# The order of the two maps in a differential attention, and a folded query scale

## The chip, the cores and the metric

The kernel runs on one core of a Trainium2 chip. The core has five engines with instruction queues of their own, each worked off in order: TensorE (PE, matrix products into PSUM), VectorE (DVE), ScalarE (ACT), GpSimd (POOL) and SyncE (SP, which here only issues DMA transfers). They wait for each other by semaphores. The metric is the device time of one launch in microseconds; a time is the median of several runs.

## The reference

Two layers of a diffusion backbone work on 512 latent tokens and 256 context tokens, each 1024 wide. Layer 0 has differential attention: 8 heads, each with two query and key parts of width 64, and the second softmax map is subtracted with a learned factor:

```python
lam = exp(sum(lp[0] * lp[1])) - exp(sum(lp[2] * lp[3])) + lam_init
o1 = sweep_attention(qq[..., 0, :], kk[..., 0, :], vv)
o2 = sweep_attention(qq[..., 1, :], kk[..., 1, :], vv)
o = rms_norm(o1 - lam * o2, subln_g) * (1.0 - lam_init)
return (o * silu(gate)) @ w_out
```

Layer 1 has grouped-query attention with 8 query heads and 2 key heads of width 128. Queries and keys go through an RMS norm per head (eps 1e-6) before rotation, and the scores are scaled by 128 ** -0.5. In both layers latent queries read latent and context keys, and context queries read context keys only. Around each mixer stand an adaLN shift, scale and gate, and norms before and after. All data are float32.

## The kernel before

The kernel keeps every product accurate by splitting each operand into a high and a low part and adding three matmuls (`mm3`: hi*hi, hi*lo, lo*hi; lines 146 to 148, or 153 for probabilities times values). ScalarE makes the high part by a cast, VectorE or POOL the low part by a subtraction.

**Layer 0.** For each of 8 heads: the projections of queries, keys, values and gate (L146 to L148) run as filling work between the attention of the head before. The attention of a head is made of score units, one for each block of 128 queries over 768 keys (`unit`), and for the two context blocks one joint unit over 256 keys (`unit_ctx`; the last head uses `unit` for them too). A unit holds two PSUM score tiles, one for each map, `sc[0]` and `sc[1]`; there are two such tiles in all, named `sc_72` and `sc_73` in the order, so the next unit can write only when the exponentials of the last have read them. Its twelve matmuls (L862, in the context unit L891) have only 64 contraction rows. Map 1 uses array rows 64 to 127 and map 0 rows 0 to 63, and the code gives them alternately, map 1 first.

Then follow, for map 0 and then map 1: the negated row maximum on VectorE (L867), the exponential with its row sum on ScalarE (L870), and the reciprocal of the sum on VectorE (L873). Map 0 is multiplied by its reciprocal on POOL (`scaled(EP0, ...)`, shown under the helper's line L208). For map 1 VectorE multiplies the reciprocal by `nlam`, the negated lambda (L877), and then computes p1 * r1 + p0 into map 0's buffer (L878). The context unit does the same in lines 897 to 909. The combined map is transposed on TensorE (L927), split into `ah` on ScalarE (L930) and `al` on VectorE (L931), and multiplied by the values (L153).

**Layer 1.** `q_proj` projects two query heads for 128 tokens at a time; `head_rstd` takes the sum of squares on ScalarE, and on POOL multiplies by 1/128, adds eps (L1270) and raises to the power of -0.5 (L1271). VectorE multiplies this by 128 ** -0.5 (L1341); the result is the per-row scale in the exponential (L1405) and of the maximum (L1402).

**What sets the order.** The generators of filling work and the steps of attention are given in an order by due times and lags (`Step`, `flow`). The framework then orders the instructions of each engine when the program is built, by priorities (`high_priority`) and by when it reckons that an instruction could start. The order is fixed from then on: at run time each engine takes its queue as it stands. A chain of order-only links (`after(prev)`) keeps the twelve matmuls of a unit in their order among themselves, but does not keep others out from between them.

Of the kernel before, what the change touches and what calls it, by code (L numbers as in the profile page):

```python
# [12 lines left out]
ALU = mybir.AluOpType  # L13
# [3 lines left out]
P = 128  # L17
# [3 lines left out]
C = 256  # L21
# [3 lines left out]
EPS = 1e-6  # L25
LAM_INIT = 0.8 - 0.6 * math.exp(0.0)
SC_A = 64 ** -0.5
SC_B = 128 ** -0.5
# [42 lines left out]
EP0 = 'p'  # L71
# [13 lines left out]
def tile_backbone(  # L85
# [20 lines left out]
    nc = tc.nc  # L106
# [97 lines left out]
    def scaled(eng, dst, src, s_):  # L204
        if eng == "a":
            nc.scalar.activation(dst, src, AF.Copy, scale=s_)
        else:
            (nc.vector if eng == "v" else nc.gpsimd).tensor_scalar(dst, src, s_, 1.0, ALU.mult, ALU.mult)  # L208
# [490 lines left out]
    with tc.tile_pool(name="t0", bufs=1) as t0:  # L699
# [140 lines left out]
        def s_units(h, qts):  # L840
            res = []

            def unit(qt):
                k0, nk = (0, T) if qt < NQ else (512, C)
                l, ps_ = small(2), []
                if nk == T:
                    sc = [sc2(), sc2()]
                else:
                    if h < KT - 1 or qt == NQ:
                        sts["sc"] = sc2()  # L850
                    sc = [sts["sc"]] * 2
                w = 384 if nk == T else 256
                qh, ql, kh_, kl_ = qk[h]
                tok = slice(qt * P, (qt + 1) * P)
                prev = None
                for j in range(nk // w):
                    c = slice(k0 + j * w, k0 + j * w + w)
                    for i, (a, b) in enumerate(((qh, kh_), (qh, kl_), (ql, kh_))):
                        for m in (1, 0):
                            r = slice(m * 64, m * 64 + 64)  # L860
                            with after(prev):
                                prev = nc.tensor.matmul(  # L862
                                    sc[m][:, j if nk == T else m, :w], a[r, tok], b[r, c], start=i == 0, stop=i == 2)
                for m in range(2):
                    scv = sc[m][:, :, :384] if nk == T else sc[m][:, m, :256]
                    mx = small()
                    nc.vector.tensor_reduce(mx, scv, AX.XY if nk == T else AX.X, ALU.max, negate=True)  # L867
                    pt = t0.tile([P, T], F32, tag=f"p{m}", name=nm("p"), bufs=4 if m == 0 else 2)[:, :nk]
                    pv_ = pt.rearrange("p (j n) -> p j n", j=2) if nk == T else pt
                    nc.scalar.activation(pv_, scv, AF.Exp, bias=mx, accum_out=l[:, m:m + 1])  # L870
                    ps_.append(pt)
                    r = l[:, m:m + 1]
                    nc.vector.reciprocal(r, r)  # L873
                    if m == 0:
                        scaled(EP0, pt, pt, r)
                    else:
                        nc.vector.tensor_tensor(r, r, nlam, ALU.mult)  # L877
                        nc.vector.scalar_tensor_tensor(ps_[0], pt, r, ps_[0], ALU.mult, ALU.add)  # L878
                        res.append(ps_[0])

            def unit_ctx():
                sc = [sc2(), sc2()]
                qh, ql, kh_, kl_ = qk[h]
                prev = None
                for qt in (NQ, NQ + 1):
                    tok = slice(qt * P, (qt + 1) * P)
                    for i, (a, b) in enumerate(((qh, kh_), (qh, kl_), (ql, kh_))):
                        for m in (1, 0):
                            r = slice(m * 64, m * 64 + 64)
                            with after(prev):  # L890
                                prev = nc.tensor.matmul(  # L891
                                    sc[m][:, qt - NQ, :C], a[r, tok], b[r, S:T], start=i == 0, stop=i == 2)
                l = [small(2), small(2)]
                pts = []
                for m in range(2):
                    mx = small(2)
                    nc.vector.tensor_reduce(mx, sc[m][:, :, :C], AX.X, ALU.max, negate=True)
                    pt = t0.tile([P, T], F32, tag=f"p{m}", name=nm("p"), bufs=4 if m == 0 else 2)
                    pts.append([pt[:, e * C:(e + 1) * C] for e in range(2)])
                    for e in range(2):  # L900
                        nc.scalar.activation(pts[m][e], sc[m][:, e, :C], AF.Exp, bias=mx[:, e:e + 1], accum_out=l[m][:, e:e + 1])
                    nc.vector.reciprocal(l[m], l[m])
                    if m:
                        nc.vector.tensor_tensor(l[m], l[m], nlam.to_broadcast([P, 2]), ALU.mult)
                    for e in range(2):
                        if m == 0:
                            scaled(EP0, pts[0][e], pts[0][e], l[0][:, e:e + 1])
                        else:
                            nc.vector.scalar_tensor_tensor(pts[0][e], pts[1][e], l[1][:, e:e + 1], pts[0][e], ALU.mult, ALU.add)
                res.extend(pts[0])  # L910

            if qts[0] == NQ and h < KT - 1:
                return res, [Step(unit_ctx, 1.0)]
            sts = {}
            cost = 1.2 if qts[0] < NQ else 0.5
            return res, [Step(lambda qt=qt: unit(qt), cost) for qt in qts]
# [97 lines left out]
        for which, o in enumerate((oq, ok)):  # L1014
            r = qr_tile()
# [222 lines left out]
    with tc.tile_pool(name="t1", bufs=1, side="right") as t1p:  # L1238
# [22 lines left out]
                    sinb[:, t, j * 64:j * 64 + 64].unsqueeze(1).to_broadcast([P, n, 64]), ALU.mult)  # L1261
            nc.gpsimd.tensor_tensor(dst.rearrange("p (h d) -> p h d", h=n), ta_, tb_, ALU.add)

        def head_rstd(o):
            ssq = small(2)
            for j in range(2):
                jk = t1p.tile([P, P], F32, tag="jk", name=nm("jk"), bufs=1)
                nc.scalar.activation(jk, o[:, j * P:(j + 1) * P], AF.Square, accum_out=ssq[:, j:j + 1])
            r = t1p.tile([P, 2], F32, tag="qrs", name=nm("qrs"), bufs=16)
            nc.gpsimd.tensor_scalar(r, ssq, 1.0 / P, EPS, ALU.mult, ALU.add)  # L1270
            nc.gpsimd.tensor_tensor(r, r, mhalf, ALU.pow)  # L1271
            return r

# [58 lines left out]
        def q_proj(p):  # L1332
            while not ws.has(2 * p, 2 * p + 1):
                yield None
            w = (ws.get(2 * p), ws.get(2 * p + 1))
            qr = []
            for m in range(NQ):
                o = pj(256)
                yield from proj_tok(o, w, m)
                qrs[p, m] = head_rstd(o)  # L1340
                nc.vector.tensor_scalar(qrs[p, m], qrs[p, m], SC_B, None, ALU.mult)  # L1341
                q = t1p.tile([P, 256], F32, tag="qt", name=nm("q"), bufs=9)
                rope_tok(q, o, m)
                close(o)
                qr.append(q)
            ws.release(2 * p, 2 * p + 1)
            qlate[p] = qr
            q_t[p] = clock[0]
# [304 lines left out]
```

## Time and profile before

| | |
|---|---|
| median of 3 runs | 853.01 us (852.29 to 855.05) |
| the profiled execution's own time | 849.65 us |
| its span, first to last instruction | 847.5 us |
| TensorE busy | 804.9 us |
| VectorE, ScalarE, POOL busy | 500.4, 457.3, 406.8 us |

In the trace the first 100 us are loading, the modulation and the first projections; 100 to 500 us are layer 0's attention with its projections; 500 to 600 us layer 0's output projection and the keys and values of layer 1; 600 to 745 us layer 1's attention with its query and gate projections; the rest is layer 1's end. A row of a timeline gives start, duration, engine, line, operation, tiles, shape and count, and in brackets the idle time of the engine before it and what ended that. Matmul durations overlap, so what a matmul takes of TensorE's queue is read from one start to the next. A row of the waits gives who waited for whom, the total in us, how often, and the longest. "wait for" is inferred from semaphore events.

### The profile page before, as it was taken

To read this page: it belongs to the slowest core of one execution; us is meant where nothing else is said; L and a number is where in the kernel's file an instruction comes from. 1 tells how busy PE (TensorE), PEld (TensorE's weight loads), DVE (VectorE), ACT (ScalarE), POOL (GpSimd) and SP (SyncE) were. 2 spreads that over 40 slices of the span, in tenths; PEclk is the share of its full clock that TensorE was granted. 3 is DMA by queue.
4 is the path that set the end of the run, shared out by engine and by line. 5 is a ranking of instruction groups with operands and counts; after the bars stand their busy time and mean duration, and the time that the engine had idled before them with its cause. 6 is when DMAs were issued, how large, how long until landed. Compare 5 with 4: busy or idle time off the path is not lost. (4 is left out here: it accounts for less than half of the span.)

```text
span 847.5 us, 14226 instructions
## 1 busy us (share of the span) xinstructions
PE 804.9 (95%) x5472; PEld 710.2 (84%) x5472; DVE 500.4 (59%) x897; ACT 457.3 (54%) x1001; POOL 406.8 (48%) x390
## 2 busy tenths in 40 slices
PE   7899999999999999999999999989999889899997
PEld 6668888788887898887988898779999779899986
DVE  4323666777667634675357952677357577665634
ACT  5323456655565635674555852565455556666731
POOL 4333555754456654555722311565777546534201
PEclk8699999999999999999999999999999999999999
DMA  9923120222142431323330043030233340210112
GB/s 301 355 96 111 67 73 27 75 75 75 38 148 77 137 101 63 112 76 100 125 100 26 26 142 107 10 123 26 75 101 100 102 147 1 75 50 26 51 49 100
DMA packets 41539, 77.76 MB, mean 92 GB/s; under 512 B 3584, under 2 KB 18688, under 8 KB 41472
## 3 DMA queue, kind: packets, MB, share of 16 engines
q1 hardware_dynamic: 38048, 71.71, 25.7%
q10 hardware_dynamic: 3424, 5.15, 1.7%
q8 instruction: 43, 0.70, 0.3%
q14 instruction: 24, 0.20, 0.1%
HBM read 70.56 MB, written 2.10 MB: 86 GB/s over the span
## 5 line engine op out<-in xcount | busy, mean ns | idle before, releaser
L146 PE MATMUL bk<-whi,h 128*128 128x256 f32 (+1 forms) x592 | 178.0, 303 | 6.5 <-DVE u L1185 3.6
L147 PE MATMUL bk<-wlo,h 128*128 128x256 f32 (+1 forms) x592 | 177.0, 300 | 0.2 <-DVE wlo L201 0.2
L148 PE MATMUL bk<-whi,h 128*128 128x256 f32 (+1 forms) x592 | 176.1, 300 | 0.7 <-DVE h L1223 0.6
L146 PE MATMUL bk<-h,whi 128*128 128x512 f32 (+2 forms) x416 | 147.6, 355 | 2.8 <-ACT sq L959 1.5
L201 POOL TENSOR_TENSOR wlo<-raw,whi 128x1024 fp32r<-128x1024 f32 x46 | 110.4, 2406 | 74.3 <-ACT whi L200 68.3
L147 PE MATMUL bk<-h,whi 128*128 128x512 f32 (+2 forms) x416 | 145.1, 349 | 0.0
L148 PE MATMUL bk<-h,wlo 128*128 128x512 f32 (+2 forms) x416 | 144.6, 348 | 0.0
L146 PEld LDWEIGHTS bk<-whi,h 128*128 128x128 f32 x592 | 113.3, 191 | 15.4 <-issue 3.6
L147 PEld LDWEIGHTS bk<-wlo,h 128*128 128x128 f32 x592 | 113.1, 191 | 5.5 <-issue 1.7
L148 PEld LDWEIGHTS bk<-whi,h 128*128 128x128 f32 x592 | 112.6, 191 | 4.9 <-DVE h L1223 1.1
L208 POOL TENSOR_SCALAR p<-p,sm 128x768 f32<-128x768 f32 (+1 forms) x80 | 67.2, 843 | 100.0 <-DVE sm L873 36.6
L146 PEld LDWEIGHTS bk<-h,whi 128*128 128x128 f32 x416 | 78.2, 188 | 16.2 <-issue 4.5
L200 ACT CAST whi<-raw 128x1024 fp32r<-128x1024 f32 x64 | 67.3, 1051 | 38.1 <-PE bk L147 21.5
L148 PEld LDWEIGHTS bk<-h,wlo 128*128 128x128 f32 x416 | 78.2, 188 | 8.5 <-issue 1.5
L147 PEld LDWEIGHTS bk<-h,whi 128*128 128x128 f32 x416 | 78.3, 188 | 7.0 <-issue 0.7
L870 ACT ACTIVATE p<-sc,sm 128x768 f32<-128x768 f32 (+1 forms) x68 | 59.5, 879 | 33.6 <-DVE sm L867 33.4
L867 DVE TENSOR_REDUCE sm<-sc 128x1 f32<-128x768 f32 (+1 forms) x68 | 60.6, 918 | 17.2 <-PE sc L862 17.1
L878 DVE SCALAR_TENSOR_TENSOR p<-p,sm,p 128x768 f32<-128x768 f32 (+1 forms) x34 | 43.5, 1280 | 14.7 <-POOL p L208 13.3
L930 ACT CAST ah<-bk 128x512 fp32r<-128x512 f32 x56 | 31.6, 591 | 35.1 <-PE bk L927 30.1
L184 POOL TENSOR_TENSOR sz<-sz,za 128x384 f32<-128x384 f32 (+1 forms) x24 | 28.4, 1183 | 40.3 <-ACT za L183 40.3
L1424 DVE TENSOR_TENSOR al<-bk,ah 128x512 fp32r<-128x512 f32 x48 | 32.3, 685 | 26.0 <-ACT ah L1423 26.0
L862 PE MATMUL sc<-qk,qk 64*128 64x384 f32 (+1 forms) x396 | 46.6, 358 | 0.8 <-POOL qk L762 0.7
(247 smaller groups left out, 1733.2 us busy)
## 6 DMA issues: line engine op xcount, KB each, us to landing
raw<-in_a_w SPq DMA_DIRECT2D x30, 512.0 KB, 3.5
araw<-in_ada_w SPq DMA_DIRECT2D x12, 1024.0 KB, 5.4
raw<-in_b_w SPq DMA_DIRECT2D x20, 512.0 KB, 3.5
ag<-in_ada_w SPq DMA_DIRECT2D x32, 256.0 KB, 6.4
raw<-in_w_out SPq DMA_DIRECT2D x16, 512.0 KB, 3.5
sw<-qr ACTq DMA_DIRECT2D x32, 128.0 KB, 2.7
raw<-in_ada_w SPq DMA_DIRECT2D x8, 512.0 KB, 3.8
xt<-in_x SPq DMA_DIRECT2D x4, 512.0 KB, 5.4
```

The lines of the kernel that those rows point to most:

```text
L146: nc.tensor.matmul(o, ahi, bhi, start=start, stop=False)
L147: nc.tensor.matmul(o, ahi, blo, start=False, stop=False)
L148: nc.tensor.matmul(o, alo, bhi, start=False, stop=stop)
L200: nc.scalar.copy(hi, r)
L201: eng.tensor_tensor(lo, r, f32(hi), ALU.subtract)
L208: (nc.vector if eng == "v" else nc.gpsimd).tensor_scalar(dst, src, s_, 1.0, ALU.mult, ALU.mult)
L862: prev = nc.tensor.matmul(sc[m][:, j if nk == T else m, :w], a[r, tok], b[r, c], start=i == 0, stop=i == 2)
L867: nc.vector.tensor_reduce(mx, scv, AX.XY if nk == T else AX.X, ALU.max, negate=True)
L870: nc.scalar.activation(pv_, scv, AF.Exp, bias=mx, accum_out=l[:, m:m + 1])
L878: nc.vector.scalar_tensor_tensor(ps_[0], pt, r, ps_[0], ALU.mult, ALU.add)
L930: nc.scalar.copy(ah, tr)
L1424: nc.vector.tensor_tensor(al, tr, f32(ah), ALU.subtract)
```

## The change

In both kinds of unit the maps are worked on in the order 1, 0 instead of 0, 1. POOL scales map 1, now with two per-row operands: the reciprocal and `nlam`. VectorE then computes p0 * r0 + p1, so that the multiplications by `nlam` (L877 and L904, 41 instructions) fall away. The matmul code is unchanged. In layer 1 the factor 128 ** -0.5 is put into the constants of POOL's first step: (128 * (ss / 128 + eps)) ** -0.5, so that L1341 (16 instructions) falls away.

```diff
-                for m in range(2):
+                for m in (1, 0):
                     scv = sc[m][:, :, :384] if nk == T else sc[m][:, m, :256]
                     mx = small()
                     nc.vector.tensor_reduce(mx, scv, AX.XY if nk == T else AX.X, ALU.max, negate=True)
...
                     r = l[:, m:m + 1]
                     nc.vector.reciprocal(r, r)
-                    if m == 0:
-                        scaled(EP0, pt, pt, r)
+                    if m == 1:
+                        nc.gpsimd.tensor_scalar(pt, pt, r, nlam, ALU.mult, ALU.mult)
                     else:
-                        nc.vector.tensor_tensor(r, r, nlam, ALU.mult)
-                        nc.vector.scalar_tensor_tensor(ps_[0], pt, r, ps_[0], ALU.mult, ALU.add)
-                        res.append(ps_[0])
+                        nc.vector.scalar_tensor_tensor(pt, pt, r, ps_[0], ALU.mult, ALU.add)
+                        res.append(pt)
...
-                for m in range(2):
+                for m in (1, 0):
                     mx = small(2)
                     nc.vector.tensor_reduce(mx, sc[m][:, :, :C], AX.X, ALU.max, negate=True)
...
-                    if m:
-                        nc.vector.tensor_tensor(l[m], l[m], nlam.to_broadcast([P, 2]), ALU.mult)
                     for e in range(2):
-                        if m == 0:
-                            scaled(EP0, pts[0][e], pts[0][e], l[0][:, e:e + 1])
+                        if m == 1:
+                            nc.gpsimd.tensor_scalar(pts[1][e], pts[1][e], l[1][:, e:e + 1], nlam, ALU.mult, ALU.mult)
                         else:
-                            nc.vector.scalar_tensor_tensor(pts[0][e], pts[1][e], l[1][:, e:e + 1], pts[0][e], ALU.mult, ALU.add)
+                            nc.vector.scalar_tensor_tensor(pts[0][e], pts[0][e], l[0][:, e:e + 1], pts[1][e], ALU.mult, ALU.add)
...
-        def head_rstd(o):
+        def head_rstd(o, fac=1.0):
...
-            nc.gpsimd.tensor_scalar(r, ssq, 1.0 / P, EPS, ALU.mult, ALU.add)
+            nc.gpsimd.tensor_scalar(r, ssq, fac / P, EPS * fac, ALU.mult, ALU.add)
             nc.gpsimd.tensor_tensor(r, r, mhalf, ALU.pow)
...
-                qrs[p, m] = head_rstd(o)
-                nc.vector.tensor_scalar(qrs[p, m], qrs[p, m], SC_B, None, ALU.mult)
+                qrs[p, m] = head_rstd(o, P)
```

The order that is built changes with it. On TensorE, in the third score unit of head 0 (`sc_73` is the score tile of map 1, `sc_72` that of map 0, `qk` the split queries and keys, `bk` a projection's PSUM bank; - is before, + is the change):

```order
 L147 MATMUL bk_71<-h_636,whi_779 128x512
 L148 MATMUL bk_71<-h_635,wlo_780 128x512
+L862 MATMUL sc_73<-qk_793,qk_791 128x384
 L146 MATMUL bk_69<-h_280,whi_779 128x256
 L147 MATMUL bk_69<-h_281,whi_779 128x256
...
 L146 MATMUL bk_69<-h_375,whi_779 128x256
 L147 MATMUL bk_69<-h_376,whi_779 128x256
-L148 MATMUL bk_69<-h_375,wlo_780 128x256
-L862 MATMUL sc_73<-qk_793,qk_791 128x384
 L862 MATMUL sc_72<-qk_793,qk_791 128x384
 L862 MATMUL sc_73<-qk_794,qk_791 128x384
```

The unit's first matmul, of map 1, has moved ahead of eight projection matmuls and stands alone there; the other eleven begin one projection matmul earlier than before. In the whole order of TensorE the 480 matmuls of L862 and L891 stand in 49 unbroken stretches before and in 83 with the change. Nearly all of this is in layer 0; in layer 1 TensorE's order is the same but for some twenty instructions.

On VectorE, at the first unit of head 0 (`sm` are the row maxima, sums and reciprocals, `p` the maps; L877 of the change is the combine that was L878):

```order
-L867 TENSOR_REDUCE sm_882<-sc_72 128x1
-L867 TENSOR_REDUCE sm_888<-sc_73 128x1
+L867 TENSOR_REDUCE sm_882<-sc_73 128x1
+L867 TENSOR_REDUCE sm_888<-sc_72 128x1
 L873 RECIPROCAL sm_869<-sm_869 128x1 x2
-L877 TENSOR_TENSOR sm_869<-sm_869,nlam 128x1
-L878 SCALAR_TENSOR_TENSOR p_884<-p_890,sm_869,p_884 128x768
...
+L877 SCALAR_TENSOR_TENSOR p_890<-p_890,sm_869,p_884 128x768
```

The reduction of map 1 comes first, so its score tile is the first to be free again; the multiplication by `nlam` is gone, and the combine follows the second reciprocal.

More of the change, by code (lines that the diff above doesn't have):

```diff
@@ L893, in unit_ctx @@
                 l = [small(2), small(2)]
-                pts = []
-                for m in range(2):
+                pts = [None, None]
+                for m in (1, 0):
                     mx = small(2)
@@ L898, in unit_ctx @@
                     pt = t0.tile([P, T], F32, tag=f"p{m}", name=nm("p"), bufs=4 if m == 0 else 2)
-                    pts.append([pt[:, e * C:(e + 1) * C] for e in range(2)])
+                    pts[m] = [pt[:, e * C:(e + 1) * C] for e in range(2)]
                     for e in range(2):
```

## The prediction

> **What bounds the kernel now.** I read the page's head and engine totals first, then the busy time by stage, then TensorE's waits in the attention stage of the first layer, and last the rows of TensorE around the score matmuls.
>
> ```profile
> span 847.5 us, 14226 instructions
> PE 804.9 (95%) x5472; PEld 710.2 (84%) x5472; DVE 500.4 (59%) x897; ACT 457.3 (54%) x1001; POOL 406.8 (48%) x390
> ...
> 100.00:500.00 400.00, 389.56 (x2724) 338.70 (x2723) 256.40 (x423) 232.88 (x489) 207.15 (x150) 0.99 0.24 78
> 600.00:745.00 145.00, 135.08 (x953) 127.93 (x952) 93.66 (x199) 82.22 (x193) 93.91 (x95) 0.99 0.28 88
> ```
>
> The last two rows give a stretch's ends, its length, and the busy us of TensorE (PE), its weight loads, VectorE (DVE), ScalarE (ACT) and GpSimd (POOL). TensorE is busy for 804.9 of 847.5 us, and for 389.6 of the 400 us in which the first layer's attention runs. The other engines have large gaps there. So this stage lasts as long as TensorE's own queue, plus 10.4 us in which TensorE waits. A change to VectorE or POOL can win only out of those 10.4 us, or out of the 9.9 us in the second layer's stage. A change that makes TensorE's queue longer costs its full length.
>
> ```profile
> PE bk L927 <- DVE al L931: 3.1, 3, 1.6
> PE bk L718 <- DVE al L931: 1.5, 1, 1.5
> PE bk L153 <- DVE al L931: 0.5, 1, 0.5
> ...
> L878 DVE SCALAR_TENSOR_TENSOR p<-p,sm,p x34: 470/1019/3140, 96.9 to 486.0; 128x768 f32<-128x768 f32 x32, 128x256 f32<-128x256 f32 x2
>   POOL p L208: 13.3, 14
> who waited for it (us, times):
> ```
>
> TensorE's waits on VectorE are for `al`, the low part of the transposed probabilities (L931). For the combine of the two maps (L878) nobody waits: the list under it is empty. The combine itself waits for POOL's scaling 14 times in 34.
>
> **The change part by part.** *The two VectorE multiplies by lambda (L877, L904) and the query scale (L1341) go.*
>
> ```profile
> L877 DVE TENSOR_TENSOR sm<-sm,nlam x34: 152/226/1899, 94.7 to 485.7; 128x1 f32<-128x1 f32 x34
> L904 DVE TENSOR_TENSOR sm<-sm,nlam x7: 161/457/1210, 126.3 to 439.1; 128x2 f32<-128x2 f32 x7
> L1341 DVE TENSOR_SCALAR qrs<-qrs x16: 147/170/703, 606.1 to 736.1; 128x2 f32<-128x2 f32 x16
> ...
> 169.83 0.99 DVE L904 TENSOR_TENSOR sm<-sm,nlam 128x2 f32<-128x2 f32 x1
> 170.75 1.28 DVE L931 TENSOR_TENSOR al<-bk,ah 128x512 fp32r<-128x512 f32 x2
> 171.48 0.66 PE L927 MATMUL bk<-ident,p 128*128 128x128 f32 x4 [1.18 <-DVE al L931]
> ...
> 482.50 0.65 DVE L877 TENSOR_TENSOR sm<-sm,nlam 128x1 f32<-128x1 f32 x1
> 483.07 0.68 DVE L931 TENSOR_TENSOR al<-bk,ah 128x512 fp32r<-128x512 f32 x1
> 713.42 0.66 DVE L1341 TENSOR_SCALAR qrs<-qrs 128x2 f32<-128x2 f32 x1
> ```
>
> Their least times are 0.15 to 0.16 us; longer ones stand still on a busy POOL or a late input, and that wait can pass to the next instruction. Nearly all are covered by TensorE's own work: VectorE is busy for 256 of 400 us. I find three places where a removed one stands directly ahead of an `al` that TensorE waits for. At 169.83 the `al` could start 0.92 us earlier, at 482.50 about 0.57 us, at 713.42 about 0.58 us: 2.1 us together, if the order there stayed. The first place is rearranged, so I take -1.5 us; the bounds are 0 and -2.1.
>
> *POOL's scaling takes lambda as a second per-row operand.* The nearest rows of POOL:
>
> ```profile
> L208 POOL TENSOR_SCALAR p<-p,sm 128x256 f32<-128x256 f32 x16 | 7.5, 481 | 14.9 <-DVE sm L902 7.8 <-DVE sm L873 7.2
> L593 POOL TENSOR_SCALAR hf<-xnt,mods 128x256 f32<-128x256 f32 x1 | 0.7, 678 | 0.0
> ```
>
> The row with two such operands (L593) took 0.20 us more than that with one at the same size. So the 48 scalings cost POOL between 0 and 9.6 us, next to 207 busy us of 400: covered. The combine that waits for them comes up to 0.2 us later, which gives back what dropping L877 (0.16 to 0.23 us) won on that chain. I take nothing. Queued behind a waiting combine on VectorE are reductions and `al`; that wait exists today (13.3 us in 14 waits) without becoming TensorE's.
>
> *The maps change places: map 1 is reduced, exponentiated and scaled first.* No instruction is added on TensorE, but its order changes. Map 1's score bank is now free first, and map 1's matmul is the first of each unit of 12. Now the built order lets that one matmul run ahead alone, with full-height matmuls between it and its 11 companions. Counted over the whole order, the 480 score matmuls stood in 49 unbroken stretches (32 of them of 12), and now stand in 83: 36 single ones and 29 of eleven among them. What a stretch costs is in the trace. They are 64 rows high; those of map 1 and map 0 run side by side. A whole one between 256-column projections:
>
> ```profile
> 198.54 0.28 PE L147 MATMUL bk<-wlo,h 128*128 128x256 f32 x1
> 198.66 0.28 PE L148 MATMUL bk<-whi,h 128*128 128x256 f32 x1
> 198.87 1.33 PE L862 MATMUL sc<-qk,qk 64*128 64x384 f32 x12
> 200.12 0.39 PE L146 MATMUL bk<-whi,h 128*128 128x256 f32 x1
> 200.35 0.28 PE L147 MATMUL bk<-wlo,h 128*128 128x256 f32 x1
> 200.47 0.29 PE L148 MATMUL bk<-whi,h 128*128 128x256 f32 x1
> ```
>
> Projections start every 0.12 us (198.54, 198.66). From 198.66 to 200.47 are 1.81 us; three projections in it take 0.36, so the twelve, which are six pairs, cost 1.45 us. Around them the starts are stretched: 0.21 instead of 0.12 going in, 0.23 instead of 0.12 after coming out. A stretch of one pair:
>
> ```profile
> 262.98 0.39 PE L148 MATMUL bk<-h,wlo 128*128 128x512 f32 x1
> 263.21 0.39 PE L146 MATMUL bk<-h,whi 128*128 128x512 f32 x1
> 263.53 0.44 PE L862 MATMUL sc<-qk,qk 64*128 64x384 f32 x2
> 263.90 0.50 PE L153 MATMUL bk<-ah,vhi 128*128 128x256 f32 x2
> 264.24 0.40 PE L153 MATMUL bk<-ah,vlo 128*128 128x256 f32 x2
> ```
>
> From 263.21 to 264.24 are 1.03 us, less 0.23 for the 512-column matmul (263.21 less 262.98) and 0.24 for two of 256 columns: 0.57 us. So six slots cost 1.45 and one costs 0.57: 0.176 us a slot, and 0.39 us for each stretch, whatever its length. A place where one unit is cut into three tests this:
>
> ```profile
> 189.39 0.28 PE L147 MATMUL bk<-wlo,h 128*128 128x256 f32 x1
> 189.60 0.61 PE L862 MATMUL sc<-qk,qk 64*128 64x384 f32 x3
> 190.14 0.44 PE L368 MATMUL bk<-sqs,ones_r 128*128 128x384 f32 x1
> 190.51 0.80 PE L862 MATMUL sc<-qk,qk 64*128 64x384 f32 x6
> 191.24 0.44 PE L369 MATMUL bk<-sqs,ones_r 128*128 128x384 f32 x1
> 191.61 0.62 PE L862 MATMUL sc<-qk,qk 64*128 64x384 f32 x3
> 192.16 0.39 PE L148 MATMUL bk<-whi,h 128*128 128x256 f32 x1
> 192.38 0.28 PE L146 MATMUL bk<-whi,h 128*128 128x256 f32 x1
> ```
>
> From 189.39 to 192.38 are 2.99 us, less 0.24 for two projections and 0.35 for L368 and L369 (384 columns, between 0.12 and 0.23): 2.40 us. Three stretches with 2, 3 and 2 slots (an odd one out has a slot of its own) should cost 3 x 0.39 + 7 x 0.176 = 2.40. It fits, and it shows that pairs form from either map, so eleven take six slots, as twelve did.
>
> The change adds 34 stretches (83 - 49) and, counted pair by pair, 33 slots (247 to 280): 34 x 0.39 = 13.3 and 33 x 0.176 = 5.8, together 19.1 us. Six of the singles are of context units with 256 columns, some 0.06 us shorter: 18.7 us. Bounds: the trace has no stretch of a single matmul, and one without a partner might cost less than a pair; if its stretch had no price, only the slots would remain, 5.8 - 0.4 = 5.4 us. Upward I find no row.
>
> Part of this falls where TensorE idles now. In the 400 us it idles 10.4 us, in 12 waits by the waits view; a single can only fill one when it stands between the transposes and the matmul that waits for them, some 3 us as I estimate it. 36 singles in 400 us put 0.27 of one in each: 12 x 0.27 x 0.57 = 1.8 us. I take -2 us; bounds 0 and -10.4.
>
> Sum: +18.7 - 1.5 - 2 = +15.2 us on the profiled execution's 849.65 us (847.5 span and 2.2 around it): 864.9. The runs' median, 853.01, lies 3.4 us above that execution, so I forecast **868 us**.
>
> The Trainium skill (TensorEngine Tiling (Array Packing), Key Properties) says that a change of tiling mode drains TensorE, which speaks against this change, and TensorE: Matmul & The Clock Gate (Step-by-step: what each phase is for) puts a drain at about 128 cycles. An estimate from that page's 2.4 GHz is 0.05 us a drain, two to a stretch, 0.11 us where the rows give 0.39; by it the sum would be 34 x 0.11 + 5.4 - 3.5 = +5.6, some 859 us. The rows decide.
>
> **The rivals.** *A: the idle time swallows more.* If all 10.4 us of waiting are filled, +18.7 - 10.4 - 1.5 = +6.8: 860 us. For it: the singles move work ahead of waits. Against it: the waits hang on chains that start on TensorE and move with it.
>
> *B: singles wait at the head of the queue.* Each stands there until map 1's exponential of the unit before is done; nothing behind it can run. If one in four (9) waited 1.1 us, the mean of the rows above being 1.0 (5.1 us in 5 waits), +10: 878 us. Against it: a unit's reduce and exponential are short next to the work between units.
>
> *C, the other side: not slower.* The price per stretch could belong to the side-by-side running: a lone matmul might not switch the array. It decides from the point where a single costs only its slot: 5.4 - 1.5 - 2 = +1.9, 855 us, no change. For it: no single is in the trace. Against it: the stretched start (0.21 for 0.12) comes ahead of the first of a stretch, before any pair is complete.
>
> *D: the change does what it says and no more.* Then only the -2.1 us of removed work and perhaps the wait at 171.48 count: 850 us. Against it: the order is not the old one.
>
> **How the numbers follow.** The forecast has 0.70, within 862 to 874 by the bounds of the two deductions; A 0.10, B 0.10, C 0.07, D 0.03. All but C and D are slower by over 0.3% (2.6 us, about what a measurement of this kernel tells from no change): slower 0.90, same 0.07, faster 0.03. The range for 8 in 10 takes in A's end and most of B: 859 to 877 us.
>
> **What would show it.** The profile after should have single L862 rows between projections, about 0.57 us of TensorE's queue each; busy TensorE should grow by some 15 us between 100 us and the end of the first layer's attention, the second layer's length should stay within 1 us, and L877's time should be gone from VectorE without TensorE's idle time there falling by more than 2 us. I am wrong if the singles come and go without stretched starts (C), if TensorE's idle time doubles in that stage (B), or if it vanishes (A).

## The result, and the profile after

The changed kernel took 860.49 us (median of 6 runs, 856.39 to 863.02) against 852.62 us for the kernel before on the same chip (6 runs, 848.83 to 855.05): a ratio of 1.0104, 95% interval 1.0074 to 1.0134. It is slower, by 8 to 9 us. (The ratio is the measured one; here and below it can differ by 0.2% from the quotient of the two medians.) The forecast had the sign and said 868 us. The measured time lies near the low end of its wide range, 859 to 877, and outside the 862 to 874 to which it gave 0.70.

The page's head and totals, and below them the busy time in the same two stretches as before (columns as there: TensorE, its weight loads, VectorE, ScalarE, POOL, the granted clock, the DMA share, GB/s):

```profile
span 856.9 us, 14181 instructions
PE 816.3 (95%) x5472; PEld 711.9 (83%) x5472; DVE 477.9 (56%) x840; ACT 456.4 (53%) x1001; POOL 414.9 (48%) x390
```

```profile
100.00:500.00 400.00, 392.88 (x2650) 332.54 (x2649) 236.56 (x374) 226.37 (x478) 211.05 (x147) 1.00 0.23 77
600.00:745.00 145.00, 136.76 (x988) 129.94 (x987) 83.35 (x177) 79.49 (x190) 92.25 (x93) 1.00 0.27 86
```

TensorE has the same 5472 matmuls and is busy 11.4 us longer (816.3 for 804.9). VectorE lost 22.5 us, and the kernel is slower all the same. In the 400 us of the attention stage TensorE is now busy for 392.9 us, so it waits 7.1 instead of 10.4 us.

The rows of TensorE around a lone score matmul, and around a stretch of eleven, in the changed kernel:

```profile
193.31 0.28 PE L146 MATMUL bk<-whi,h 128*128 128x256 f32 x1
193.43 0.28 PE L147 MATMUL bk<-wlo,h 128*128 128x256 f32 x1
193.64 0.44 PE L862 MATMUL sc<-qk,qk 64*128 64x384 f32 x1
194.01 0.39 PE L148 MATMUL bk<-whi,h 128*128 128x256 f32 x1
194.23 0.28 PE L146 MATMUL bk<-whi,h 128*128 128x256 f32 x1
...
219.25 0.40 PE L153 MATMUL bk<-al,vhi 128*128 128x256 f32 x2
219.58 1.31 PE L862 MATMUL sc<-qk,qk 64*128 64x384 f32 x11
220.82 0.50 PE L153 MATMUL bk<-ah,vhi 128*128 128x256 f32 x2
221.16 0.40 PE L153 MATMUL bk<-ah,vlo 128*128 128x256 f32 x2
```

From 193.43 to 194.23 are 0.80 us; two projections take 0.24, which leaves 0.56 for the one. From 219.25 to 221.16 are 1.91 us; two L153 of 256 columns ahead and two behind take 4 x 0.12, which leaves 1.43 us for the eleven. The same working over all undisturbed places of the trace gives these medians:

| stretch of score matmuls | before | after |
|---|---|---|
| twelve, 384 columns | 1.446 us (21 places) | too few |
| eleven, 384 columns | none | 1.437 us |
| one alone, 384 columns | none | 0.566 us (26 places) |
| one alone, 256 columns | none | 0.513 us (5 places) |

So each unit that is split pays 0.56 us more, and the prediction's 0.57 and 0.51 stand as they were.

TensorE's waits in the same 400 us of the changed kernel (what waited, for what; us in total, times, longest):

```profile
PE sc L862 <- ACT p L870: 1.8, 3, 0.7
PE bk L153 <- DVE al L928: 1.2, 3, 0.7
PE bk L924 <- DVE al L928: 1.1, 1, 1.1
PE bk L146 <- DVE gT L208: 0.9, 1, 0.9
```

Before, 5.1 us were spent on `al` (three rows, five waits). Now it is 2.5 us with the small one at L731. New is the first row: the score matmuls wait for an exponential (L870), three times, 1.8 us.

POOL's scaling with lambda as a second operand stands beside the one-operand form in the same trace:

```profile
L875 POOL TENSOR_SCALAR p<-p,sm,nlam 128x768 f32<-128x768 f32 x32 | 33.4, 1044 | 50.6 <-DVE sm L873 49.0 <-DVE mods L417 1.5
L208 POOL TENSOR_SCALAR p<-p,sm 128x768 f32<-128x768 f32 x32 | 30.1, 941 | 47.7 <-DVE sm L1402 29.1 <-DVE sm L1398 18.6
```

It costs 0.10 us each, 3.3 us over the 32 of this size, on an engine that is idle for nearly half of the stage (busy for 211 of 400 us).

**Where the time went.** I divide the first layer's attention (from the first score matmul to the last transpose of a map) into three parts. The *stretches* are the score matmuls with the change of mode around them, measured as above; the *waits* are TensorE's idle time; the *rest* is everything else on TensorE, including what it loses at half clock. The last column is the number of 3.4 us periods with a granted clock of a half in that stage.

| run | stage, us | stretches: number, us | waits, us | rest, us | half-clock periods |
|---|---|---|---|---|---|
| before | 401.1 | 49, 59.2 | 10.4 | 331.5 | 2 |
| after | 411.3 | 83, 78.3 | 7.1 | 325.8 | 0 |

The stretches grew by 19.1 us, where I had forecast 18.7. But 3.3 us of waits and 5.7 us of the rest went, so the stage grew by only 10.1 us. (It also began 2.8 us earlier, at 85.2 for 88.0 us, and 2.0 us were added behind it, so the span grew by 9.4.) The totals of the stretches use a median where a place is disturbed, and are good to about 1 us. The half-clock periods are part of that rest. The kernel before had its two behind the wait at 171.48 that the prediction shows (1.18 us) and behind this one:

```profile
444.58 0.68 PE L927 MATMUL bk<-ident,p 128*128 128x128 f32 x4 [1.56 <-DVE al L931]
```

Busy time and granted clock (0.50 and 0.51, the third number from the end) in the windows behind them, in the kernel before

```profile
172.00:175.40 3.40, 3.40 (x18) 2.84 (x20) 3.40 (x4) 0.75 (x2) 3.40 (x2) 0.50 0.12 16
445.00:448.40 3.40, 3.40 (x19) 3.18 (x18) 2.65 (x8) 0.85 (x3) 0.90 (x1) 0.51 0.02 5
```

and in the same windows of the changed one:

```profile
172.00:175.40 3.40, 3.40 (x26) 3.40 (x25) 3.21 (x5) 2.20 (x4) 1.64 (x3) 1.00 0.00 0
445.00:448.40 3.40, 3.40 (x27) 3.01 (x26) 2.69 (x6) 3.26 (x8) 0.00 (x0) 1.00 0.47 147
```

In 3.4 us at a clock of 0.50 TensorE did 18 or 19 matmuls; at full clock it does 26 or 27 there (not the same ones). By the stretched starts inside them the two cost about 1.5 and 1.2 us. That is about half of the 5.7 us that went from the rest.

The rest also holds a second kind of stretch. The matmuls that make the second layer's modulation (L718) use TensorE in tiles of 32 columns (`128*32`), and the built order puts them into unbroken stretches too. A stretch of two, in the experiment with less work:

```profile
299.31 0.28 PE L146 MATMUL bk<-whi,h 128*128 128x256 f32 x1
299.51 1.04 PE L718 MATMUL bk<-araw,s 128*32 128x512 f32 x2
300.49 0.39 PE L147 MATMUL bk<-wlo,h 128*128 128x256 f32 x1
300.71 0.28 PE L148 MATMUL bk<-whi,h 128*128 128x256 f32 x1
```

and one of eight, in the changed kernel:

```profile
310.34 0.28 PE L148 MATMUL bk<-whi,h 128*128 128x256 f32 x1
310.55 1.07 PE L718 MATMUL bk<-araw,s 128*32 128x512 f32 x8
311.55 0.39 PE L146 MATMUL bk<-whi,h 128*128 128x256 f32 x1
311.77 0.28 PE L147 MATMUL bk<-wlo,h 128*128 128x256 f32 x1
```

Less 0.24 us for two projections, the two take 1.16 us and the eight 1.19 (median of 78 undisturbed stretches of eight in eleven profiles: 1.19). So each stretch costs about 1.2 us, whether it holds a whole group of eight or a piece of one. The kernel before has 13 of them and the change 12: another 1.2 of the 5.7 us. I haven't placed the last 1.8 us.

### The profile page after: what moved, and what is told of

It reads as the page before. It is cut to its first block, busy times and chain, and to the rows that moved or that the text cites. A ratio compares the mean times of both kernels' runs of the same rounds, so it can differ in the third digit from the quotient of the medians.

```text
span 856.9 us, 14181 instructions
## 1 busy us (share of the span) xinstructions
PE 816.3 (95%) x5472; PEld 711.9 (83%) x5472; DVE 477.9 (56%) x840; ACT 456.4 (53%) x1001; POOL 414.9 (48%) x390
## 5 line engine op out<-in xcount | busy, mean ns | idle before, releaser
L201 POOL TENSOR_TENSOR wlo<-raw,whi 128x1024 fp32r<-128x1024 f32 x46 | 112.3, 2446 | 62.7 <-ACT whi L200 60.6
L146 PEld LDWEIGHTS bk<-whi,h 128*128 128x128 f32 x592 | 112.7, 191 | 13.5 <-DVE u L1182 3.2
L870 ACT ACTIVATE p<-sc,sm 128x768 f32<-128x768 f32 (+1 forms) x68 | 59.9, 881 | 30.4 <-DVE sm L867 30.3
L875 POOL TENSOR_SCALAR p<-p,sm,nlam 128x768 f32<-128x768 f32 (+1 forms) x34 | 34.5, 1016 | 54.8 <-DVE sm L873 53.2
L862 PE MATMUL sc<-qk,qk 64*128 64x384 f32 (+1 forms) x396 | 58.7, 362 | 2.3 <-ACT p L870 1.8
L877 DVE SCALAR_TENSOR_TENSOR p<-p,sm,p 128x768 f32<-128x768 f32 (+1 forms) x34 | 46.5, 1368 | 18.0 <-POOL p L875 16.5
L862 PEld LDWEIGHTS sc<-qk,qk 64*128 64x128 f32 x396 | 38.0, 184 | 18.6 <-issue 7.6
L208 POOL TENSOR_SCALAR p<-p,sm 128x768 f32<-128x768 f32 x32 | 30.1, 941 | 47.7 <-DVE sm L1402 29.1
L928 DVE TENSOR_TENSOR al<-bk,ah 128x512 fp32r<-128x512 f32 x56 | 37.7, 685 | 17.9 <-ACT ah L927 17.6
```

Of the source, the lines that this page charges most:

```text
L146: nc.tensor.matmul(o, ahi, bhi, start=start, stop=False)
L201: eng.tensor_tensor(lo, r, f32(hi), ALU.subtract)
L862: prev = nc.tensor.matmul(sc[m][:, j if nk == T else m, :w], a[r, tok], b[r, c], start=i == 0, stop=i == 2)
L875: nc.gpsimd.tensor_scalar(pt, pt, r, nlam, ALU.mult, ALU.mult)
L877: nc.vector.scalar_tensor_tensor(pt, pt, r, ps_[0], ALU.mult, ALU.add)
L928: nc.vector.tensor_tensor(al, tr, f32(ah), ALU.subtract)
```

## The experiments

My theory after the result: the loss is the lone matmuls and nothing else, each at its full 0.57 us of queue, and about half of it is given back because waits and half-clock periods shrink. The ten kernels below were run on three chips, each beside the kernel before on the same chip (850.33 us median for the four that move the lone matmul or close the units, 849.67 for the fold, the doses and the change again, 850.59 for the last two). All times are ratios to it.

### Is it the lone matmul? Three ways of moving it

The change, but with map 0's matmul first in each pair, so that the first matmul of a unit is not the one whose bank comes free first (here and in the next, the same edit stands in the context unit too):

```diff
-                        for m in (1, 0):
+                        for m in (0, 1):
```

> The change, but with the score matmuls of each unit given map 0 first, so that the first matmul of a unit needs the score tile that comes free last. In the built order the 480 score matmuls stand in 52 unbroken stretches (before: 49, the change: 83). Theory of the stretches: the loss goes away; 3 stretches and 2 slots more than before are 3 x 0.39 + 2 x 0.18 = 1.5 us, against up to 2 us of VectorE relief, so 849 to 854 us, as before. Rival, that POOL's second operand or the later combine costs the time: nothing of that is undone here, so 859 to 862 us as the change. Rival, that any order with map 1 first has worse waits: also near 860 us.

Measured: 850.75 us, ratio 1.0008 (0.9980 to 1.0036). With all but two of the 36 lone matmuls gone (52 stretches) the loss is gone, while the lambda on POOL, the combine in its new place and the folded scale are all still there.

The kernel before with the same word edited the other way, `for m in (0, 1)` in place of `(1, 0)`, and nothing else of the change:

> The kernel before with one thing changed, the score matmuls of each unit given map 0 first; maps, lambda and query scale as before. This is the mirror of the change: now map 0 is worked on first and its matmul leads. The order has 82 stretches and 281 slots. Theory of the stretches: TensorE's queue grows by 33 x 0.39 + 34 x 0.176 = 18.9 us, of which about half shows, as it did in the change: 860 to 864 us. Rival of POOL and the combine: nothing of that is changed, so 852 to 853 us.

Measured: 860.18 us, ratio 1.0109 (1.0089 to 1.0129). The whole loss comes from one word in a kernel that has none of the change. Its profile has the lone matmul with the same stretched starts:

```profile
220.84 0.40 PE L153 MATMUL bk<-al,vhi 128*128 128x256 f32 x2
221.16 0.43 PE L862 MATMUL sc<-qk,qk 64*128 64x384 f32 x1
221.53 0.50 PE L153 MATMUL bk<-ah,vhi 128*128 128x256 f32 x2
221.87 0.40 PE L153 MATMUL bk<-ah,vlo 128*128 128x256 f32 x2
```

From 220.84 to 221.87 are 1.03 us; four L153 take 0.47; 0.56 is left for the one.

The kernel before with the maps' order changed in the reductions, exponentials and scalings, but lambda still multiplied on VectorE and no second operand on POOL:

```diff
-                for m in range(2):
+                for m in (1, 0):
...
-                    if m == 0:
-                        scaled(EP0, pt, pt, r)
+                    if m == 1:
+                        nc.vector.tensor_tensor(r, r, nlam, ALU.mult)
+                        scaled(EP0, pt, pt, r)
```

> The kernel before with the maps worked on in the order 1, 0, but lambda still multiplied into the reciprocal on VectorE (the two small instructions remain) and the query scale as before. The order has 80 stretches and 279 slots. Theory of the stretches: 31 x 0.39 + 32 x 0.176 = 17.7 us more of queue, 859 to 864 us. Rival of POOL's second operand: 852 to 853 us, since POOL scales with one operand as before.

Measured: 865.34 us, ratio 1.0163 (1.0127 to 1.0198). So POOL's second operand isn't needed for the loss. The median is 1.3 us above the expected 859 to 864 us; the six runs lie between 859.95 and 868.51.

### The folded scale alone

```diff
-                qrs[p, m] = head_rstd(o)
-                nc.vector.tensor_scalar(qrs[p, m], qrs[p, m], SC_B, None, ALU.mult)
+                qrs[p, m] = head_rstd(o, P)
```

> The kernel before with only the second layer's part of the change: the query scale goes into the variance constants, the 16 small VectorE multiplies (L1341) go, and the first layer is untouched (49 stretches of score matmuls, 247 slots, as before). Both theories: between 0 and -0.6 us, the one place where TensorE waited behind such a multiply (0.58 us); no change that can be told, ratio 0.998 to 1.002. Below 0.997 would mean that this part hides a gain inside the whole change's loss.

Measured: 849.22 us, ratio 1.0009 (0.9984 to 1.0033). No difference that can be told, and no hidden gain.

### A test that did not test it: the units as closed pieces

The change, with the twelve score matmuls of a unit placed as one piece that nothing may interrupt, instead of as a chain:

```diff
-                            with after(prev):
-                                prev = nc.tensor.matmul(
+                with tc.tile_critical():
...
+                                nc.tensor.matmul(
```

> The change, matmul order as in it (map 1 first), but the twelve score matmuls of a unit are scheduled as one piece, so that nothing stands between them: 41 stretches and 246 slots. Theory of the stretches: 8 stretches fewer than before are -3.3 us, and the change's relief of up to 2 us comes on top: 846 to 851 us. Rival of POOL and the combine: 857 to 862 us. Rival, that the early single matmul helped by freeing work: slower than the change.

Measured: 898.09 us, ratio 1.0566 (1.0536 to 1.0595). The expectation was wrong. The number of stretches was the lowest of all (41), but the pieces bring waits of their own. Two places in TensorE's rows of that kernel:

```profile
196.36 1.32 PE L861 MATMUL sc<-qk,qk 64*128 64x384 f32 x12 [0.43 <-ACT za L181]
...
206.08 1.32 PE L861 MATMUL sc<-qk,qk 64*128 64x384 f32 x12 [0.44 <-issue]
```

and its waits from 85 to 530 us, the two largest:

```profile
PE sc L861 <- issue: 5.7, 13, 0.4
PE sc L861 <- POOL qr L754: 4.4, 1, 4.4
```

TensorE stands idle for some 0.4 us ahead of many pieces, and a few times for 3 to 4 us, as in the second row: its waits in the stage are 49 us instead of 7. One of the rivals in the expectation, that the early single matmul helped, had forecast a slower kernel too; but with map 0 first nearly all of them were gone at no cost. The run says what this way of keeping a unit whole costs, and nothing on the lone matmuls.

### Why only half? The same dose, with and without a change of mode

The stage took up about half of what was added. Either any added work is taken up so, or a mode change's price overlaps with something. Two doses of nearly the same length, in the kernel without lone matmuls (the first one above), are put ahead of each of the 34 units of `unit`, about where the lone matmuls of the change stood (the context units get none); they write map 1's bank, which the scores overwrite:

```diff
+                for _ in range(3):
+                    nc.tensor.matmul(sc[1][:, 0 if nk == T else 1, :w], qh[:, tok], kh_[:, k0:k0 + w], start=True, stop=True)
```

> The changed kernel with map 0's matmul first in each pair (so no lone matmul: 49 stretches, 249 slots), and ahead of each unit's scores three extra full-height matmuls (128 rows, the unit's own operands, 384 or 256 columns) into map 1's score bank, which the first score matmul then overwrites. In the built order they run ahead of the unit exactly as the lone matmuls of the change did, at 34 places, but they don't change TensorE's mode. By the rows they lengthen TensorE's queue by 32 x 3 x 0.174 + 2 x 3 x 0.118 = 17.4 us, less 1.2 for three stretches fewer: +16.2. Theory 1 (the lone matmuls cost their full 0.57 us of queue, and about half of ANY work added in this stage disappears in waits and slow-clock stretches that get shorter): about +8 us on the kernel without lone matmuls, ratio to the kernel before 1.007 to 1.012. Theory 2 (plain work costs its whole length here, and part of a mode change's price is an overlap that costs nothing): +16 us, ratio 1.017 to 1.021.

```diff
+                nc.tensor.matmul(sc[1][:, 0 if nk == T else 1, :w], qh[64:128, tok], kh_[64:128, k0:k0 + w], start=True, stop=True)
```

> As the plain dose, but instead of three full-height matmuls one extra 64-row matmul of map 1 without a partner, ahead of each unit at 34 places: 78 stretches and 284 slots against 52 and 249 of the kernel without it. By the rows this lengthens TensorE's queue by 26 x 0.39 + 35 x 0.176 = 16.3 us, the same dose as the plain one (+16.2), now with mode changes. Theory 1: the same as the plain dose within 3 us, about +8, ratio to the kernel before 1.007 to 1.012. Theory 2: clearly less than the plain dose, +6 to +9 against its +16.

The whole change again, beside them:

> The whole change once more, beside the two doses on one chip: 83 stretches and 280 slots, +18.7 us of queue against before. Theory 1: ratio 1.008 to 1.013, and a profile in which the first layer's attention is about 10 us longer than before's, with TensorE's waits there some 3 us less. Theory 2 has the same number for this kernel; only its ratio to the plain dose differs.

Measured: plain dose 860.19 us, ratio 1.0141 (1.0102 to 1.0179); lone dose 854.53 us, 1.0056 (1.0029 to 1.0082); the change 860.46 us, 1.0147 (1.0112 to 1.0181). The doses are in the profiles, though of the 34 lone ones only 29 stand alone and five join other score matmuls. A plain one:

```profile
192.95 0.28 PE L148 MATMUL bk<-whi,h 128*128 128x256 f32 x1
193.07 0.69 PE L857 MATMUL sc<-qk,qk 128*128 128x384 f32 x3
193.60 0.28 PE L146 MATMUL bk<-whi,h 128*128 128x256 f32 x1
```

Three full-height matmuls take 0.53 us (193.07 to 193.60) without stretched starts. A lone one takes 0.566 us here too (median of the places in the lone dose's trace).

The two doses came out 5.7 us apart, where theory 1 allowed 3, so its expectation failed in that point. Its ratios were off as well: it had 1.007 to 1.012 for both doses, and the plain one came out above that, the lone one below; the change came out above its 1.008 to 1.013. Theory 2's 1.017 to 1.021 was too high for the plain dose. (The measured intervals reach into all of these ranges.) That the lone dose cost clearly less is what theory 2 had said. But that theory needed the lone kind to be cheap as such, and there it falls: the change itself, 83 stretches with 36 lone matmuls, cost on the same chip as much as the plain dose. That both doses shorten the waits is seen in the same three parts as above:

| run | stage, us | stretches (with the dose), us | waits, us | rest, us | half-clock periods | ratio |
|---|---|---|---|---|---|---|
| fold alone | 402.4 | 59.8 | 12.6 | 330.1 | 1 | 1.0009 |
| change, map 0 first | 403.7 | 62.1 | 11.2 | 330.4 | 3 | 1.0008 |
| lone dose | 408.9 | 76.8 | 4.9 | 327.2 | 0 | 1.0056 |
| plain dose | 414.4 | 79.1 | 6.5 | 328.9 | 1 | 1.0141 |
| change again | 412.3 | 78.6 | 6.4 | 327.3 | 1 | 1.0147 |
| before, matmuls swapped | 414.0 | 77.5 | 6.2 | 330.3 | 1 | 1.0109 |
| before, order only | 411.0 | 76.9 | 6.1 | 328.0 | 1 | 1.0163 |

Against the kernel with map 0 first, the stretches of the plain dose are 17.0 us longer and those of the lone dose 14.7 (I had reckoned 16.2 and 16.3). The doses' stages differ by 5.5 us: 2.3 in the stretches, 1.6 in the waits, 1.7 in the rest. The rest has one half-clock period and 14 stretches of L718 with the plain dose, none and 13 with the lone one, which is enough for the 1.7. These are single profiles; which waits a given order has is partly chance, and I don't claim more for the 5.7 us than that.

Over all: three kernels with about the old number of stretches (before and the first two rows) have waits of 10.4 to 12.6 us and a rest of 330.1 to 331.5. The six with some 16 to 19 us more of TensorE work (after and the last five rows) have waits of 4.9 to 7.1 and a rest of 325.8 to 330.3. By their means +17.5 us of work comes out as +9.6: -5.2 in waits and -2.8 in the rest (rounded).

### More of it, and less of it

If it is a stock of waits, a second dose should find it nearly used up. The plain dose with `range(6)` for `range(3)`:

> The plain dose twice: six extra full-height matmuls ahead of each unit instead of three, at 34 places; 50 stretches, 248 slots. TensorE's queue by the rows: +34 us on the kernel without lone matmuls (which measured as the kernel before, 850 us). The single plain dose had +17 us of queue and gave +10.5 us of time; TensorE's waits in the stage fell from 11 to 6.5 us and the slow-clock time from three stretches to one. Theory 1a (a small stock of waits and slow-clock time is used up, about 6 to 8 us, and then work costs its whole length): +26 to +28 us, ratio 1.030 to 1.034, waits of 4 to 6 us left in the stage. Theory 1b (a fixed share, some 40%, of any added work goes): +20 us, ratio 1.022 to 1.026.

Measured: 873.84 us, ratio 1.0272 (1.0241 to 1.0304). Stage 427.1 us, stretches with doses 95.5, waits 5.5, rest 326.1, no half-clock period. Of the first dose's 17.0 us the stage had kept 10.7; of the second's 16.4 it kept 12.7. So the share that disappears falls (37%, then 23%), but no sharp floor is reached: the ratio's interval touches both forecasts, and neither is settled by it. Of the second dose's missing 3.7 us only 1.0 came from waits and 2.8 from the rest, while the last half-clock period of the stage went. L718 sharpens the picture. It has 12 stretches with map 0 first, 14 with the plain dose and 13 with the double one; at 1.2 us each the first dose really put 19.4 us into the queue and the second 15.2, and 45% and then 16% of that disappeared.

Less work, with the third product term of the scores left out in the kernel with map 0 first (its scores are less exact, so it is no replacement for either kernel):

```diff
-                    for i, (a, b) in enumerate(((qh, kh_), (qh, kl_), (ql, kh_))):
+                    for i, (a, b) in enumerate(((qh, kh_), (qh, kl_))):
```

> The other direction: the changed kernel with map 0's matmul first in each pair, and of the three product terms of the scores the third (low part of q by high part of k) left out, so eight score matmuls a unit instead of twelve; the scores are less exact, the rest is computed as before. 46 stretches and 164 slots against 52 and 249: 6 x 0.39 + 85 x 0.176 = 17.3 us less in TensorE's queue. Theory 1a (the waits are chains through VectorE, ScalarE and POOL of fixed length that TensorE's work covers, so that less work uncovers them): waits in the stage rise from 11 to 16 us or more, the time falls by 9 to 13 us, ratio 0.985 to 0.990. Rival (the waits move with TensorE's own work and keep their length, as the prediction argued): the time falls by the whole 17 us, ratio 0.979 to 0.981, waits 10 to 12 us.

Measured: 840.03 us, ratio 0.9868 (0.9839 to 0.9898). The stretches are 17.0 us shorter than with map 0 first (45.1 for 62.1), as worked out, and the stage only 9.7 us (394.0): the time is where theory 1a put it. But the waits rose to 12.7 us only, not to 16. The rest rose by 5.8 us, to 336.2, with as much half-clock time as there (10.2 us). Most of that is L718 again: its matmuls stand in 15 stretches here and in 12 with map 0 first, about 3.6 us of the 5.8. So this order took back by chance a part of the 17 us, and the waits gave back only 1.5. One long wait with half clock behind it stands in this kernel's rows (granted clock 0.50 from 262.6 to 269.4 us):

```profile
263.91 1.12 PE L924 MATMUL bk<-ident,p 128*128 128x128 f32 x4 [3.06 <-DVE al L928]
264.67 0.78 PE L146 MATMUL bk<-h,whi 128*128 128x512 f32 x1
265.25 0.63 PE L147 MATMUL bk<-h,whi 128*128 128x512 f32 x1
265.68 0.63 PE L148 MATMUL bk<-h,wlo 128*128 128x512 f32 x1
266.10 0.63 PE L146 MATMUL bk<-h,whi 128*128 128x512 f32 x1
```

After a wait of 3.06 us for `al` the 512-column matmuls start 0.43 us apart (265.25, 265.68, 266.10), against 0.23 in the prediction's rows at full clock.

None of these kernels computes the whole reference and beats the kernel before.

## Why the prediction was right, and where it was not

**What bounds the kernel.** Right. 22.5 us less on VectorE bought nothing; with TensorE's order left nearly as it was (map 0 first) the change measured 1.0008, and a plain dose on TensorE alone cost 1.4%.

**The removed VectorE work, -1.5 us.** Not refuted and not shown. The kernel with map 0 first has three stretches more than the one before, 2.9 us by the trace, and came out level; the fold alone is level too. The part is below what these runs tell. L877's 15.9 us and L904's 4.0 went without a gain that these runs could tell.

**POOL's second operand, nothing.** Right: 0.10 us each, 3.3 us of POOL, and the order alone, without the second operand, was slow as well. The combine's wait for POOL did grow (13.3 to 16.3 us), and no matmul of TensorE stood behind it; two weight loads waited 0.5 us.

**The order on TensorE, +18.7 us.** Right in number and in cause: 0.566 us for a lone matmul against 0.57, 0.513 against 0.51, 19.1 us in all. One edited word takes the loss away or brings it. With the estimate from the Trainium skill's drain (TensorE: Matmul & The Clock Gate, Step-by-step), 0.11 us for a stretch, the 34 new stretches and 33 slots would have added 9.1 us of queue, and the trace has 19.1. That its 859 us lies near the measured 860.5 is two errors that meet: a price too low by half, and nothing like the deduction that the stage really makes.

**The deduction for idle time, -2 us: the term that was mis-sized.** It measured about -9 us in the profile after (3.3 in waits; 5.7 in the rest, of which about 2.7 are the two half-clock periods and 1.2 the stretch of L718 that is gone) and about -8 as the mean of six kernels. Two reasonings in it failed. First, I asked only whether a lone matmul stands between the transposes and the matmul that waits for them. But the waits shrank with any work that was added to TensorE's queue: a plain dose did the same as the lone matmuls. My reading, that a wait for `al` ends on ScalarE's and VectorE's work of fixed length and is covered by work ahead of it, fits that, but is not shown: with 17 us less work the waits grew by only 1.5 us. Secondly, I priced a wait at its own length, though in the two windows quoted above a wait of 1.2 to 1.6 us was followed by a further 1.2 to 1.5 us lost at half clock. The bound I had set, -10.4, was the waits alone. The -9 stays inside it partly by luck, since more than half of it is not waits.

**The inner range.** I gave 0.70 to 862 to 874 us "by the bounds of the two deductions". By those bounds (0 to -2.1, 0 to -10.4) it is 853.0 + 18.7 less 0 to 12.5: 859 to 872. The measured 860.5 lies in this one and not in the one that I wrote.

**The base.** I added the sum to 853.0 us, the median of three runs; in the four sets of runs since, before's median was 849.7 to 852.6. That is 0.4 to 3.3 us of the 7.5 by which 868 was too high.

**The rivals.** A (the idle time swallows more, 860 us) came nearest, in its time and in its direction: the waits fell, though to 7.1 and not to 0, and half-clock time and L718 gave up some 4 us more. I had given it 0.10. B (lone matmuls wait at the queue's head) exists, as the three waits for an exponential, 1.8 us where I had put 10. C is refuted by the 0.566 us, D by the order.

**The signs I had named.** Lone L862 rows with stretched starts: there. TensorE's busy time in the stage +15 us: by the stage's length less its waits it is 404.2 against 390.7, +13.5. L877 gone without TensorE's waits falling by more than 2 us: missed, they fell by 3.3. The second layer's length within 1 us: missed, since from the end of the first layer's attention to the end the trace went from 358.4 to 360.4 us. The fold isn't the cause, being level by itself; the half-clock time in that part of the program went from 3.4 to 10.2 us (3.4 and 6.8), beside the period at the very end that all profiles have.

## What to carry to other kernels

Before changing which of two results is consumed first, look at which matmul heads the unit that produces them: when its bank is the one that comes free first, a scheduler may send it ahead alone, and where the unit runs TensorE in another tiling than its neighbours, each such split is paid in full (0.56 us here, 34 times). On a kernel bound by one engine, price added work in that engine's queue exactly, but expect the time to move by less than the queue (here +17 us gave about +10 in the mean of six kernels): waits close and half-clock periods go. Then count every kind of stretch in the new order, and not only the one that was moved: with less work -17 us gave only -10, and 3.6 of the missing 7 were L718's. And let the matmul that is free first be second in its pair: one word was worth 1%.

## What the runs showed of the hardware beyond that

**Half-clock periods follow short waits.** In the profiles of the kernel before, the change and nine of the experiments (all but the closed pieces), 36 periods at a granted clock of a half, 3.4 or 6.8 us long, begin between 80 and 780 us of the span. Ahead of 35 of them TensorE had a wait of at least 0.9 us that ended less than 3.5 us earlier or was still running; ahead of the other one it had waited 0.49 and 0.25 us around eight two-column matmuls. The reverse does not hold: of 96 such waits only 36 were followed by one, and a wait of 3.4 us in the second layer had none in the kernel before. The Trainium skill (TensorE: Matmul & The Clock Gate, Part 1: The HAM clock gate) has the clock drop after an idle window of about 3.4 us, in windows that run free of the program; the length of the periods agrees, but here single waits of 1.1 to 1.6 us stood ahead of several periods, with at most 0.7 us of other waits near them. That the waits cause the periods is read from their order in time, and no run here tested it by itself.

**A lone matmul of half height pays the whole change.** 0.566 us alone, 1.437 us for eleven, 1.446 us for twelve: the twelfth costs nothing because six pairs and five pairs with one left over take the same slots, and the fixed 0.39 us doesn't care how many follow. Single places in the profiles of the change and the lone dose agree: five took 1.02 us and six 1.02, seven took 1.20 and eight 1.21.

**Narrow tiles too.** A stretch of 32-column matmuls (L718) took 1.2 us with two matmuls in it and 1.2 with eight.
